# Layer 1's projections, scores and compressed scores in two scaled F16 parts instead of two F32R parts

## The chip, the cores and the metric

The kernel runs on one core of a Trainium2 chip. The metric is the device time of one execution in microseconds; the time of a kernel is the median of its runs. One further execution is recorded by the profiler, and the profile's page and trace are of that one.

The core's engines run side by side, each in its own order, and wait for each other by semaphores: PE (matmul; its weight loads are listed as PEld), DVE (vector), ACT (activation functions and scaled copies), POOL (a second, general vector engine) and SP, which here issues the DMAs. PE writes only into PSUM, eight banks of 128 partitions x 512 F32 numbers; DVE and ACT empty them.

## The reference

Two layers over x of 1024 positions and 1024 channels, each `x <- x + W_out(mixer(RMSNorm(x)) * silu(z))`, then a final RMSNorm. Layer 0 is an attention with a forget gate (16 heads of 64 channels, causal). Layer 1, the one that is changed, has 16 query heads in 4 groups that share keys and values, and three branches, mixed by a sigmoid gate:

```
proj = h @ w_in                  # q, and kc, vc, ks, vs, kw, vw of 4 x 64 each, 48 gates, z
kc, vc = compress(kc_raw), compress(vc_raw)          # 63 blocks, a small MLP with silu
p_c = softmax(mask(rope(q) . rope(kc) * 64**-0.5));  o_c = p_c @ vc
imp = overlap-sum of p_c over a group's heads;       idx = the 8 best blocks of 64 keys
o_s = softmax(rope(q) . ks over the chosen blocks) @ vs
o_w = softmax(rope(q) . kw over the last 512 keys) @ vw
y = ((g0*o_c + g1*o_s + g2*o_w) * silu(z)) @ W_out
```

## The kernel before

**Precision by parts.** A matrix product here is made of two parts of each operand: the high part is the value rounded to the product's type, the low part is what is left. `mm3` (line 134) issues three matmuls, high x high, high x low, low x high, one behind the other. In layer 0 and in layer 1's projections the parts are F32R, a form in which PE takes 32-bit operands in one pass. The products of the probabilities with the values are in F16 parts already.

**Layer 0** (to some 560 us). `merge` (line 212) interleaves two generators by costs written beside each step: the main one scores, softmaxes and multiplies tiles of 128 queries (`FoxDuo`), the fill projects the next head pair (`fox_k`, `fox_v`, `fox_q`, `fox_z`). Scores run two duos ahead of their products with the values; in between lies a DMA transpose of the probabilities.

**The passage** (some 560 to 640 us). `out_rest0` finishes the output projection for the last head pair, adds, normalizes with `gB` (the norm's gain) and writes the transposed h in its two parts, `hT` (`to_hT`, line 112), which layer 1's projections read.

**Sections** (some 610 to 960 us). Layer 1's weights are 28 sections of 1024 x 128: kc, qa, qr, vc, v, ka, kr, and z (8). `next_w` (line 777) loads two sections ahead through `load_w` (line 123): a DMA into a staging tile `wst` (one buffer), a cast to the high part on DVE, four subtractions for the low part on POOL. `section` (line 785) runs `project`, 24 matmuls of 512 columns a half, two halves, and hands each PSUM bank to a `use` function that empties it. q and k go as two stacked parts of 64 rows to DRAM (`qD`, `kD`, through `put_split`, line 901); `cmp_raw` keeps the raw compressed input in SBUF, `cmp_mlp` (line 818) makes the compressed keys `kcm` and values `vb`. `nsa_fill` (line 1156) lists the sections; `cmp_main` (line 1104) runs beside it by `merge`: 16 `cmp_unit`s (line 1057), each with 8 products of 128 columns, two DVE passes that add the mask, 8 exponentials, the block choice.

**Layer 1's attention** (some 960 to 1410 us). 32 `NsaSuper`s (16 heads x 2 halves of the queries). A `unit` (line 1320) makes one score tile of 128 queries: up to 1024 keys for the chosen blocks (y = 0), up to 640 for the window (y = 1). PE writes it (line 1343), DVE adds the mask and takes the row's minimum in one instruction (line 1350; the scores are negated), ACT takes the exponential (line 1353). The chosen blocks' probabilities are transposed by PE (line 1375) and split by ACT and DVE (lines 152 and 153), the window's are split on POOL (lines 1356, 1357) and transposed by DMA. PE multiplies both with the values (lines 1383 to 1385). The z sections and the first part of the output projection are the fill.

The order on each engine follows the program's order where the planner finds a step ready, and lets a later one go first where it doesn't.

## Time and profile before

| | us |
|---|---|
| median of 3 runs | 1480.85 (1480.15 to 1482.15) |
| span of the profiled execution | 1477.9 |
| PE / PEld busy in it | 1402.7 / 1164.1 |
| DVE / ACT / POOL busy | 1064.7 / 805.7 / 594.0 |
| moved by DMA | 243.13 MB, 165 GB/s mean |

In the profile, a row of a group has the line, the engine, the operation, what it writes and reads, the shape, the count, then the busy time, the mean duration of one in ns, and the idle time before it with what ended it. A timeline row begins with the start in us from the span's start and the duration; rows of the same kind may be merged (x4). A PE duration is from the first column to the modelled end, so two that follow each other overlap; the distance between starts says what one costs. Windows give each engine's busy time in a stretch, its instructions in brackets, then the granted clock of PE, the share of the DMA engines and GB/s.

### The profile page before, as it was taken

How to read it: one execution, taken by the hardware profiler on the slowest of the kernel's cores; microseconds unless marked ns; L12 is line 12 of the kernel's file. 1: busy time of each engine (PE TensorE's matmuls, PEld its weight loads, DVE VectorE, ACT ScalarE, POOL GpSimd, SP SyncE). 2: the span in 40 equal slices, each digit the busy share in tenths (PEclk: the TensorE clock that was granted, in tenths of full speed). 3: DMA queues.
4: the chain of work that ended last, by engine and by line, in shares of the span. 5: the costliest groups of instructions: out<-in, count | busy, mean ns of one | idle time of the engine just before them, and what ended most of it. 6: DMA issues, size and time to landing. Idle time of an engine off the chain costs nothing.

```text
span 1477.9 us, 29812 instructions
## 1 busy us (share of the span) xinstructions
PE 1402.7 (95%) x10488; PEld 1164.1 (79%) x10488; DVE 1064.7 (72%) x2795; ACT 805.7 (55%) x2030; POOL 594.0 (40%) x781
## 2 busy tenths in 40 slices
PE   5999999999999898999999988989999999989998
PEld 4888888888888676877788867778888888877876
DVE  6586778787787787666554658768788878878744
ACT  5365646565565644344132565566676676766523
POOL 2233232333233220123433334357676766766400
PEclk9999999999999999999999998999999999999999
DMA  6886867877867987442525577686786786877534
GB/s 244 264 167 138 181 136 170 174 158 164 175 140 161 219 199 150 141 155 71 166 85 151 171 185 180 185 201 144 155 180 155 160 177 147 172 201 166 105 137 147
DMA packets 405557, 243.13 MB, mean 165 GB/s; under 512 B 332640, under 2 KB 352736, under 8 KB 405152
## 3 DMA queue, kind: packets, MB, share of 16 engines
q1 hardware_dynamic: 405408, 241.23, 67.9%
q8 instruction: 83, 1.36, 0.4%
q14 instruction: 66, 0.54, 0.1%
HBM read 121.36 MB, written 44.11 MB: 112 GB/s over the span
## 4 chain that ended last, share of the span: by engine, by line
PE 69%; DVE 13%; DMA 6%; ACT 6%; issue 3%; SPq 2%; POOL 1%; DVEq 0%; ACTq 0%; POOLq 0%
PE S_n L1343 6%; PE y L135 3%; PE ptp_n L1375 3%; PE y L137 3%; PE y L136 3%; PE k L135 2%; PE v L135 2%; PE k L136 2%; PE k L137 2%; PE S L597 2%; PE S L598 2%; PE v L137 2%; PE v L136 2%; PE O L631 2%; PE q L135 2%
## 5 line engine op out<-in xcount | busy, mean ns | idle before, releaser
L1353 ACT ACTIVATE P_n<-P_n,m_n 128x640 f32<-128x640 f32 (+7 forms) x256 | 187.4, 733 | 67.7 <-DVE m_n L1352 41.0
L615 ACT ACTIVATE P<-P,m 128x512 f32<-128x512 f32 (+1 forms) x192 | 116.8, 609 | 129.8 <-DVE m L606 128.9
L1343 PE MATMUL S_n<-nk,nq 128*128 128x320 f32 (+5 forms) x768 | 177.1, 345 | 11.0 <-DVE m_n L1350 7.9
L586 POOL TENSOR_TENSOR Bd<-B,tri 128x128 f32<-128x128 f32 x128 | 62.0, 500 | 232.8 <-DVE m L606 224.7
L1357 POOL TENSOR_TENSOR hl_n<-P_n,hl_n 128x640 f16<-128x640 f32 (+4 forms) x128 | 142.6, 1114 | 9.4
L1343 PEld LDWEIGHTS S_n<-nk,nq 128*128 128x128 f32 x768 | 125.0, 190 | 24.7 <-DVE m_n L1350 10.7
L617 DVE SCALAR_TENSOR_TENSOR hl<-P,hl 128x512 f16<-128x512 f32 (+1 forms) x192 | 114.7, 616 | 16.0 <-ACT hl L616 14.9
L1350 DVE CUSTOM_DVE_ANT_0 P_n<-S_n,wmask 128x640 f32<-128x640 f32 (+2 forms) x192 | 113.0, 595 | 18.4 <-PE S_n L1343 15.0
L1356 POOL CAST hl_n<-P_n 128x640 f16<-128x640 f32 (+4 forms) x128 | 75.2, 587 | 115.6 <-ACT P_n L1353 104.6
L152 ACT ACTIVATE pth_n<-ptp_n 128x512 f16<-128x512 f32 (+1 forms) x160 | 86.6, 546 | 55.2 <-PE ptp_n L1375 54.0
L153 DVE SCALAR_TENSOR_TENSOR ptl_n<-ptp_n,pth_n 128x512 f16<-128x512 f32 (+1 forms) x160 | 100.6, 634 | 18.5 <-ACT pth_n L152 17.0
L135 PE MATMUL y<-wo,ohi 128*128 128x512 f32 x230 | 93.9, 408 | 3.1 <-ACT ohi L499 1.4
L1375 PE MATMUL ptp_n<-ident,P_n 128*128 128x128 f32 x576 | 90.7, 278 | 5.7 <-DVE ptl_n L153 3.7
L616 ACT ACTIVATE hl<-P 128x512 f16<-128x512 f32 (+1 forms) x192 | 92.4, 513 | 2.3 <-DMA pT<-hl 1.0
L137 PE MATMUL y<-wo,olo 128*128 128x512 f32 x230 | 90.7, 394 | 0.0
L136 PE MATMUL y<-wo,ohi 128*128 128x512 f32 x230 | 90.2, 392 | 0.0
L1375 PEld LDWEIGHTS ptp_n<-ident,P_n 128*128 128x128 f32 x576 | 66.0, 141 | 19.0 <-DVE ptl_n L153 12.3
L1350 DVE CUSTOM_DVE_ANT_0 P_n<-S_n,bias 128x640 f32<-128x640 f32 (+1 forms) x64 | 65.2, 1018 | 9.8 <-PE S_n L1343 9.7
L1383 PE MATMUL O_n<-nv,pth_n 128*128 128x64 f16 x576 | 70.3, 195 | 0.5
L597 PE MATMUL S<-KH,Q 128*128 128x512 f32 (+1 forms) x192 | 64.2, 350 | 6.2 <-DVE m L606 6.2
L1384 PE MATMUL O_n<-nv,pth_n 128*128 128x64 f16 x576 | 69.5, 193 | 0.0
L1385 PE MATMUL O_n<-nv,ptl_n 128*128 128x64 f16 x576 | 68.5, 193 | 0.0
(395 smaller groups left out, 4543.9 us busy)
## 6 DMA issues: line engine op xcount, KB each, us to landing
nq<-qD SPq DMA_DIRECT2D x64, 256.0 KB
B<-cD SPq DMA_DIRECT2D x16, 512.0 KB
wo<-wD SPq DMA_DIRECT2D x16, 512.0 KB
nq<-qD SPq DMA_DIRECT2D x64, 128.0 KB
x<-in_x_dram SPq DMA_DIRECT2D x8, 512.0 KB
wst_k<-in_fox_w_dram SPq DMA_DIRECT2D x8, 512.0 KB
wst_v<-in_fox_w_dram SPq DMA_DIRECT2D x8, 512.0 KB
wD<-in_fox_w_out_dram SPq DMA_DIRECT2D x8, 512.0 KB
```

The source lines that it names most:

```text
L135: T.matmul(ps, wh, mh, start=first, stop=False, **kw)
L136: T.matmul(ps, wh, ml, start=False, stop=False, **kw)
L137: T.matmul(ps, wl, mh, start=False, stop=last, **kw)
L153: V.scalar_tensor_tensor(lo[:, 0:n], pt[:, 0:n], scale, h, OP.mult, OP.subtract)
L597: T.matmul(ps[:, 0:n], q, KH[j][:, k0:k0 + n], start=True, stop=False)
L615: A.activation(L[:, 0:n], L[:, 0:n], AF.Exp, bias=init, scale=-1.0, accum_out=self.lr[:, col + c:col + c + 1])
L617: V.scalar_tensor_tensor(lo[:, cs], L[:, 0:n], UP, hi[:, cs], OP.mult, OP.subtract)
L1343: T.matmul(ps[:, b, 0:w], self.q[x][:, qi * P:(qi + 1) * P], k[:, k0 + b * w:k0 + b * w + w], start=(x == 0), stop=(x == 1))
L1350: V.tensor_tensor_reduce(dst, src, mk, 1.0, 3e38, OP.add, OP.min, m)
L1353: A.activation(L, L, AF.Exp, bias=m, scale=-1.0, accum_out=self.l[:, y, qi:qi + 1])
L1357: G.tensor_tensor(hl[:, n:2 * n], L, hl[:, 0:n], OP.subtract)
L1375: T.transpose(pt[:, (x + i) * P:(x + i + 1) * P], L[:, kb * P - k0:(kb + 1) * P - k0], ident)
```

## The change

Layer 1's h, its projection weights, q, k, the compressed keys and the gate's weights become two F16 parts. F16 has a small range, so each group of weights (kc, vc, q, gate, then k, v, z) is first multiplied by a power of two that is derived from the sum of the group's squares; the norm's gain is scaled likewise, and the inverse factors go into the steps that empty PSUM, into the masks and into the exponentials.

- The sums of squares: `Squares` loads weights once more from DRAM, squares them on ACT and accumulates. `early` (25 tiles, of 512 columns at most, one buffer) steps after each half of `fox_q` and `fox_z` in layer 0; `late` (16 tiles of 1024 columns, two buffers) after each half of a section in layer 1. `step` first makes a [128, 1] copy that reads a tile of the surrounding work, so that the square can't run before it.
- `roots` adds the sums over the partitions by a small matmul with ones, and cuts the result to a power of two with integer operations on DVE. It runs after layer 0's attention, once more before the fifth qr section (`late_scales`), and once for the compressed keys, with a step of 2200 between their square and the root.
- `load_w` scales the staged weights in place on ACT, between the DMA and the cast; every second section is staged in another pool.
- The masks use 2**126 in place of 1e30.

```diff
+    class Squares:
...
+        def step(self, x):
+            if self.at:
+                t, col = self.at.pop(0)
+                z = consts.tile([P, 1], F32, tag="zg", bufs=2, name=f"zg_{col}")
+                A.activation(z, x, AF.Copy, scale=0.0)
+                A.activation(t, t, AF.Square, bias=z, accum_out=sums[:, col:col + 1])
+            self.load()
+
+    def roots(groups, name, parts=P):
...
+        for i, x in enumerate(groups):
+            V.tensor_reduce(r[:, 0, i:i + 1], x, AX.X, OP.add)
+        V.tensor_copy(tb[:, 0:n], r[:, 0])
+        V.tensor_copy(tb[:, n:2 * n], r[:, 0])
+        pt = ps_t(f"total_{name}")
+        T.matmul(pt[:, 0:2 * n], ones, tb, start=True, stop=True)
+        V.tensor_scalar(r[:, 0].bitcast(I32), pt[:, 0:n].bitcast(I32), 24, 23,
+                        OP.logical_shift_right, OP.logical_shift_left)
+        V.tensor_scalar(r[:, 1].bitcast(I32), r[:, 0].bitcast(I32), 0x3F800000, None, OP.bitwise_xor)
+        return r
...
-    def load_w(pool, src, name, cols=P):
-        st = pool.tile([P, KC, cols], F32, tag="wst", bufs=1, name=f"wst_{name}")
+    def load_w(pool, src, name, scale=None, staged=None):
+        st = (staged or pool).tile([P, KC, P], F32, tag="wst", bufs=1, name=f"wst_{name}")
         dma(st, src)
-        hi = pool.tile([P, KC, cols], F32R, tag="whi", bufs=2, name=f"whi_{name}")
-        lo = pool.tile([P, KC, cols], F32R, tag="wlo", bufs=2, name=f"wlo_{name}")
+        dt = F32R if scale is None else F16
+        hi = pool.tile([P, KC, P], dt, tag="whi", bufs=2, name=f"whi_{name}")
+        lo = pool.tile([P, KC, P], dt, tag="wlo", bufs=2, name=f"wlo_{name}")
+        if scale is not None:
+            A.activation(st, st, AF.Copy, scale=scale)
         V.tensor_copy(hi, st)
...
             ready["q", p, half] = Q
+            early.step(f(q[:, 0:1]))
...
             ready["z", p, half] = zs
+            early.step(z[:, 0:1])
...
     merge(fox_main(), fox_fill(), PACE, rebase=True, cap=4000)
+    r1 = roots([sums[:, 0:4], sums[:, 4:8], sums[:, 8:24], sums[:, 24:25]], "early")
...
         dma(gB, a["norm_g"][1:2, :].to_broadcast([P, D]))
+        gain.extend(gain_scale(gB))
...
-    hT = [[h1.tile([P, KC, 512], F32R, tag=f"h{x}{i}", name=f"hT1_{x}_{i}") for i in range(2)] for x in range(2)]
+    hT = [[h1.tile([P, KC, 512], F16, tag=f"h{x}{i}", name=f"hT1_{x}_{i}") for i in range(2)] for x in range(2)]
...
-    qD = dram.tile([H, 2, P, 512], F32, name="qD")
-    kD = dram.tile([8, P, S], F32, name="kD")
+    qD = dram.tile([H, 2, P, 512], F16, name="qD")
+    kD = dram.tile([8, P, S], F16, name="kD")
...
                 pts.append(use(half, pt, len(pts)))
+                late.step(pt[:, 0:1])
+
+    late = Squares(pa, [(a["nsa_w"][i], 13 + i) for i in range(12, 28)], D, 2)
...
-                A.copy(R[0:64, g, half * 512:half * 512 + 512], pt[r, :])
+                A.activation(R[0:64, g, half * 512:half * 512 + 512], pt[r, :], AF.Copy, scale=E[kind][r])
...
+            A.activation(t2, t1, AF.Square, accum_out=ks[0:64])
+            yield 2200
+            r = roots([ks], "kcm")
...
-        V.tensor_tensor(L, sc[:, :, :, 1, :], cmask[:, t0:t0 + 2, None, :].to_broadcast([P, 2, 4, 64]), OP.add)
-        V.tensor_tensor(L, sc[:, :, :, 0, :], L, OP.add)
+        uc = ready["uc"]
+        for y in range(2):
+            V.scalar_tensor_tensor(L[:, y], sc[:, y, :, 1, :], uc, cmask[:, t0 + y, None, :].to_broadcast([P, 4, 64]),
+                                   OP.mult, OP.add)
+        V.scalar_tensor_tensor(L8, sc.rearrange("p y r a c -> p (y r) a c")[:, :, 0, :], uc, L8, OP.mult, OP.add)
...
-            V.tensor_tensor_reduce(dst, src, mk, 1.0, 3e38, OP.add, OP.min, m)
+            unit, minus = ready["units"][0:2]
+            V.tensor_tensor_reduce(dst, src, mk, 1.0 if y else unit, 3e38, OP.add, OP.min, m)
             if y:
-                V.tensor_scalar(m, m, LNUP, None, OP.add)
-            A.activation(L, L, AF.Exp, bias=m, scale=-1.0, accum_out=self.l[:, y, qi:qi + 1])
+                V.tensor_scalar(m, m, unit, LNUP, OP.mult, OP.add)
+            A.activation(L, L, AF.Exp, bias=m, scale=minus if y else -1.0, accum_out=self.l[:, y, qi:qi + 1])
```

More of the change, by code (lines that the diff above doesn't have):

```diff
@@ L30 @@
 BIG = 1e30
+FAR = 2.0 ** 126
 SCALE = HD ** -0.5
@@ L74, in tile_fox_nsa, with silu2 @@
     G.memset(zero, 0.0)
+    ones = consts.tile([P, P], BF16, name="ones")
+    G.tensor_copy(ones, warm.to_broadcast([P, P]))
     wp = ctx.enter_context(tc.tile_pool(name="wp", bufs=2))
     ready = {}
-    def silu2(dst, src):
-        A.activation(dst, src, AF.Tanh, scale=0.5)
+    def silu2(dst, src, scale=0.5):
+        A.activation(dst, src, AF.Tanh, scale=scale)
         V.scalar_tensor_tensor(dst, dst, 1.0, src, OP.add, OP.mult)
@@ new lines, in roots @@
+    def roots(groups, name, parts=P):
+        n = len(groups)
+        r = consts.tile([P, 4, n], F32, name=f"roots_{name}")
+        tb = consts.tile([P, 2 * n], BF16, name=f"sb_{name}")
+        for i, x in enumerate(groups):
[8 more added lines that the diff above has]
+        return r
@@ new lines, in gain_scale @@
+    def gain_scale(gB):
+        u = consts.tile([P, 4], F32, name="gain")
+        m, r, e, b = (u[:, i:i + 1] for i in range(4))
+        V.tensor_reduce(m, gB, AX.X, OP.max, apply_absolute_value=True)
+        V.tensor_scalar(m, m, 2.0 ** -60, None, OP.max)
+        V.tensor_scalar(m.bitcast(I32), m.bitcast(I32), 0x7F800000, None, OP.bitwise_and)
+        V.tensor_scalar(r.bitcast(I32), m.bitcast(I32), 0x7F800000, None, OP.bitwise_xor)
+        V.tensor_scalar(gB, gB, r, 2.0 ** 8, OP.mult, OP.mult)
+        V.tensor_scalar(e, m, 2.0 ** -9, None, OP.mult)
+        V.tensor_scalar(b, r, 2.0 ** 15, 2.0, OP.min, OP.mult)
+        return e, b
@@ L743, in tile_fox_nsa, with scales, bound @@
     out_rest0(ow, ready["wout"], after0)
+    W, E = {}, {}
+    def scales(r, kinds, name):
+        V.tensor_scalar(r[:, 2], r[:, 1], 2.0 ** 77, None, OP.mult)
+        V.tensor_scalar(r[:, 3], r[:, 0], gain[0], 2.0 ** 50, OP.mult, OP.mult)
+        for i, x in enumerate(kinds):
+            W[x], E[x] = r[:, 2, i:i + 1], r[:, 3, i:i + 1]
+    def bound(n, e, sign, name):
+        u = consts.tile([P, 2], F32, name=f"bound_{name}")
+        V.tensor_scalar(u[:, 0:1], n, 2.0 ** 68, 2.0 ** 25, OP.mult, OP.min)
+        V.tensor_tensor(u[:, 0:1], u[:, 0:1], gain[1], OP.mult)
+        V.tensor_scalar(u[:, 1:2], u[:, 0:1], e, sign, OP.mult, OP.mult)
+        return u[:, 0:1], u[:, 1:2]
+    scales(r1, ("kc", "vc", "q", "g"), "early")
+    rq, eq = bound(r1[:, 1, 2:3], E["q"], -1.0, "q")
     ow.release()
@@ L793, in section, with late_scales @@
                 pts.append(use(half, pt, len(pts)))
+                late.step(pt[:, 0:1])
+    late = Squares(pa, [(a["nsa_w"][i], 13 + i) for i in range(12, 28)], D, 2)
+    late.load()
+    def late_scales():
+        r = roots([sums[:, 25:29], sums[:, 29:33], sums[:, 33:41]], "late")
+        scales(r, "kvz", "late")
+        rk, ek = bound(r[:, 1, 0:1], E["k"], 1.0, "k")
+        u = pers.tile([P, 4], F32, name="units")
+        inverse(u[:, 0:1], rq, rk, SCALE)
+        V.tensor_scalar(u[:, 1:2], u[:, 0:1], -1.0, None, OP.mult)
+        V.tensor_scalar(u[:, 2:3], E["z"], 0.5, None, OP.mult)
+        V.tensor_tensor(u[:, 3:4], E["z"], E["v"], OP.mult)
+        ready["units"] = [u[:, i:i + 1] for i in range(4)]
+        ready["ek"] = ek
     pm = tc.alloc_tile_pool(name="pm", bufs=1, reuse_waits="tile")
@@ L954, in use @@
             x = rt(f"kx_{half}")
-            A.copy(x, pt)
+            A.activation(x, pt, AF.Copy, scale=ready["ek"])
             rope(x[0:64], x[64:128], rows[0], rows[1], 64, 1.0, half, k_dst, "k")
@@ L1009, in gate_sec @@
                 yield 430
-            A.copy(gT[half], pt[64:112, :])
-            V.tensor_tensor(gT[half], pt[0:48, :], gT[half], OP.add)
+            A.activation(gT[half], pt[64:112, :], AF.Copy, scale=E["g"][64:112])
+            V.scalar_tensor_tensor(gT[half], pt[0:48, :], E["g"][0:48], gT[half], OP.mult, OP.add)
         pt = ps_t("pgt")
@@ L1044, in load_q12 @@
         if (h, s) not in Q12:
-            q = [kv[1 - s].tile([P, 512], F32R, tag=f"nq{i}", name=f"nq{i}_{h}_{s}") for i in range(2)]
-            dma(f(q[0]), qD[h, s])
+            q = [kv[1 - s].tile([P, 512], F16, tag=f"nq{i}", name=f"nq{i}_{h}_{s}") for i in range(2)]
+            dma(q[0], qD[h, s])
             for i in range(2):
-                dma(f(q[1][rows[i], :]), qD[h, s, rows[1 - i], :])
+                dma(q[1][rows[i], :], qD[h, s, rows[1 - i], :])
             Q12[h, s] = q
```

87 lines of the change are left out of this document (57 added, 30 removed).

## The prediction

> **What bounds the kernel now.** I read the page from the top, then busy time by stage, then the chain of waits, then TensorE's instructions one by one. A busy share says little of PE here, because the records of two matmuls overlap; the last of these views decides.
>
> ```profile
> span 1477.9 us, 29812 instructions
> ...
> PE 1402.7 (95%) x10488; PEld 1164.1 (79%) x10488; DVE 1064.7 (72%) x2795; ACT 805.7 (55%) x2030; POOL 594.0 (40%) x781
> ...
> PE 69%; DVE 13%; DMA 6%; ACT 6%; issue 3%; SPq 2%; POOL 1%; DVEq 0%; ACTq 0%; POOLq 0%
> ```
>
> The first two lines are the busy times; the third, the chain that ended last, goes through PE for 69% of the span. By stage (start:end, then PE, PEld, DVE, ACT, POOL busy, clock, DMA share, GB/s):
>
> ```profile
> 90.00:540.00 450.00, 442.88 (x2787) 363.84 (x2784) 347.62 (x1066) 255.54 (x638) 143.03 (x223) 0.99 0.78 169
> 540.00:640.00 100.00, 91.52 (x541) 73.74 (x539) 72.09 (x177) 45.80 (x116) 12.05 (x20) 1.00 0.59 154
> 640.00:800.00 160.00, 155.63 (x773) 129.91 (x772) 85.46 (x150) 49.71 (x78) 58.92 (x75) 0.99 0.38 117
> 800.00:960.00 160.00, 147.25 (x724) 121.30 (x722) 109.92 (x255) 87.43 (x344) 60.97 (x77) 0.97 0.65 179
> 960.00:1410.00 450.00, 430.11 (x5052) 364.44 (x5052) 361.41 (x965) 301.78 (x712) 294.63 (x349) 1.00 0.75 162
> ```
>
> These are layer 0's attention, the passage between the layers, layer 1's first sections, its later sections with the compressed scores, and layer 1's attention. What a wide matmul costs PE is the step from start to start (start, duration, engine, line, ...):
>
> ```profile
> 596.28 0.39 PE L135 MATMUL y<-wo,ohi 128*128 128x512 f32 x1
> 596.51 0.39 PE L136 MATMUL y<-wo,ohi 128*128 128x512 f32 x1
> ...
> 607.61 0.39 PE L137 MATMUL y<-wo,olo 128*128 128x512 f32 x1
> ```
>
> From 596.28 to 607.61 lie 50 steps, so 227 ns for 512 columns, with no hole. Where such steps follow each other, PE is the limit, and only a shorter step helps. If I give each of the 773, 724 and 5052 matmuls of the last three rows the step that its form shows back to back, the steps fill some 97%, 89% and 90% of these stages. So the changed part of the program is bound by PE's order, except around the compressed scores.
>
> **The change, part by part.** Half the width of an operand does not halve the step: 0.44 ns a column is already one column after another. What F16 costs is seen in the kernel's own F16 products:
>
> ```profile
> 302.52 0.23 PE L631 MATMUL O<-v,pT 128*128 128x128 f16 x1
> 302.58 0.19 PE L632 MATMUL O<-v,pT 128*128 128x64 f16 x1
> 302.61 0.22 PE L631 MATMUL O<-v,pT 128*128 128x128 f16 x1
> ...
> 1152.47 0.19 PE L1384 MATMUL O_n<-nv,pth_n 128*128 128x64 f16 x1
> 1152.49 0.19 PE L1385 MATMUL O_n<-nv,ptl_n 128*128 128x64 f16 x1
> 1152.52 0.48 PE L135 MATMUL nz<-hT,whi_nz 128*128 128x512 f32 x1
> 1152.84 0.40 PE L136 MATMUL nz<-hT,whi_nz 128*128 128x512 f32 x1
> 1153.07 0.40 PE L137 MATMUL nz<-hT,wlo_nz 128*128 128x512 f32 x1
> ```
>
> 128 and 64 columns take 60 and 30 ns, weight load included. No F16 product of 512 columns stands in the trace, so its step is bounded: four times the F16 step of 128 columns (57 to 60 ns) is no gain at all, 213 ns (a gain of 14) if the whole extra of the F32 step is not per column. I take a gain of 8 ns. The Trainium skill, "TensorE: Matmul & The Clock Gate", section "Back-to-back issue gap", gives 518 cycles for 512 columns, 216 ns; by it the gain would be 11 ns and the sum below 4 us shorter. The same section's other figure, 131 ns sustained at 512, disagrees with the 227 ns here; it is a rival below.
>
> The second gain is larger. The nz product at 1152.52 follows short ones, and its successor starts 320 ns later in place of 227: its F32 weights could not be loaded behind a matmul of 30 ns. F16 weights are loaded at every 30 ns step above. The same shows in the scores, first behind a wide product, then behind a transpose:
>
> ```profile
> 999.99 0.76 PE L1343 MATMUL S_n<-nk,nq 128*128 128x320 f32 x4
> ...
> 1151.47 0.85 PE L1343 MATMUL S_n<-nk,nq 128*128 128x320 f32 x4
> ...
> 971.61 0.47 PE L1343 MATMUL S_n<-nk,nq 128*128 128x448 f32 x1 [0.41 <-DVE m_n L1350]
> ...
> 1391.81 0.70 PE L1343 MATMUL S_n<-nk,nq 128*128 128x512 f32 x2
> ...
> 957.44 0.47 PE L135 MATMUL nz<-hT,whi_nz 128*128 128x512 f32 x1
> ...
> 1317.91 0.48 PE L135 MATMUL nz<-hT,whi_nz 128*128 128x512 f32 x1
> ```
>
> The same four matmuls take 0.85 in place of 0.76. I count 124 such scores (first and last: the third and fourth line) and 94 such nz products (the last two), 18.6 us together. Scores of 128 columns (64 of them in attention, 128 compressed ones) also pay for the F32 load, about 107 ns a step:
>
> ```profile
> 817.95 1.00 PE L1063 MATMUL sc<-kcm,nq 128*128 128x128 f32 x8
> 818.79 0.45 PE L135 MATMUL pn_v<-hT,whi_nv 128*128 128x512 f32 x1
> ```
>
> Eight in 0.84 us, 105 each, against 57.
>
> *Attention, 960 to 1410.* Offered on PE: 18.6 of loads, 704 scores x 8 ns = 5.6, 64 narrow ones x 50 = 3.2, z products 384 x 8 = 3.1: 30.5 us, 7% of the stage. Against it stands DVE. Its mask-and-minimum for the chosen blocks gets a per-partition scalar, and so does the small step behind the window's. What such an operand costs is shown by layer 0's same instruction with and without one:
>
> ```profile
> L606 DVE CUSTOM_DVE_ANT_0 P<-S,Bd,m 128x128 f32<-128x128 f32 x84 | 27.4, 348 | 1.8
> ...
> L606 DVE CUSTOM_DVE_ANT_0 P<-S,Bd 128x128 f32<-128x128 f32 x27 | 7.7, 284 | 1.7 <-PE S L598 1.6
> ```
>
> 64 ns, so 256 x 0.06 = 15 us: DVE goes from 361 to 377 us of work. With all 30.5 us saved that would be 90% of the stage, and DVE is already full in parts of every round of heads:
>
> ```profile
> 1126.00:1132.00 6.00, 6.00 (x79) 5.53 (x78) 6.00 (x14) 4.75 (x10) 4.80 (x5) 1.00 0.46 87
> ...
> 1230.00:1236.00 6.00, 6.00 (x79) 5.56 (x78) 6.00 (x14) 4.77 (x10) 4.81 (x5) 1.00 0.39 58
> ```
>
> DVE is busy 6.00 of 6.00. In those parts a faster PE only waits for its score banks. I take 70% of the offer: **-21** (from -8 to -31).
>
> *Sections, 640 to 960.* 20 sections of 48 products and the gate's 32 x 8 ns = 7.9, the compressed scores 128 x 48 ns = 6.2. Part of it falls where PE already waits for the softmax of the compressed scores; the compressed score's two DVE passes become three with scalars, 16 x some 0.3 us in that chain. I take half: **-7**. New on ACT: each section's weights are multiplied by their scale (1024 columns), and 16 squares of 1024 columns; per instruction:
>
> ```profile
> L94 ACT ACTIVATE h_n<-xr 128x512 f32<-128x512 f32 x32 | 20.0, 626 | 29.7 <-DVE xr L1476 16.5 <-DVE xr L720 12.9 <-DVE st_n L102 0.4
> ...
> L94 ACT ACTIVATE h_n<-x 128x1024 f32<-128x1024 f32 x8 | 8.5, 1060 | 4.6 <-DMA x<-in_x_dram 4.6
> ...
> L985 ACT ACTIVATE nvT<-nvT,nvsc 128x512 f32<-128x512 f32 x8 | 5.5, 716 | 8.6 <-DVE nvsc L179 8.6
> L986 ACT CAST nvs<-nvT 128x512 f16<-128x512 f32 x8 | 4.7, 609 | 1.3 <-DMA nv<-nvs 1.3
> ```
>
> 1.06 us for 1024 columns, and 107 ns more with a scalar per partition (716 against 609). 20 x 1.17 + 16 x 1.4 is 46 us on an engine with 183 us idle in these 320; it lies beside PE. Where it is ahead of an eviction or a compression input in ACT's order, PE waits a little: **+2** (0 to +10). Behind a square, SP's next load waits for its buffer; the weights have a second staging buffer now, which takes that wait away. The late roots' matmul waits on DVE in PE's order, but the squares it needs end two sections before. The compressed key's new square and root (some 3 us) have one section's products put between them.
>
> *Layer 0.* 25 squares of 512 columns: 0.63, about 0.19 for the accumulator read and 0.2 for the ordering copy, 25 us on ACT, which is idle for 195 of the 450. Each ordering copy waits for a q or z tile that DVE finishes; behind it on ACT stand the exponentials of the running scores. 25 loads of 256 KB are 6.5 MB, 9% more than the stage moves (169 GB/s x 450 us), and each load waits on SP for the square before it (one buffer), with the probabilities' transposes behind it on SP; those have two tiles' time to land. **+3** (0 to +25).
>
> *Passage.* The first roots (nine tiny DVE steps) and the gain's scale (some 3 us of DVE) lie where DVE idles; the products and the ACT scaling ahead of layer 1's first weights can show: **+1.5** (0 to +6).
>
> *At nothing:* q and k in F16 halve two kinds of load, 64 x 256 and 64 x 128 KB,
>
> ```profile
> nq<-qD SPq DMA_DIRECT2D x64, 256.0 KB
> ...
> nq<-qD SPq DMA_DIRECT2D x64, 128.0 KB
> ```
>
> which are ahead of their use in nearly all rounds; the cover is the round before. The masks and the windows' exponentials with a second scalar (128 x 0.1 us) lie on ACT, idle for a third of the stage.
>
> The sum: -21 - 7 + 2 + 3 + 1.5 = -21.5, on the median of 1480.85 (the span is 1477.9, some 3 us of each run lie outside it and don't change): **1459 us**.
>
> **Rivals.** *All of it:* the wide step gains 11 to 14 ns and DVE keeps up: -31 - 14 and some 8 for the step, nothing added: about 1428. For it: PE's chain share; against it: DVE's full windows. *DVE takes over:* attention gives 8 us only, the sum is 1472; for it DVE at 84% of the old stage and full in bursts; against it, it is idle for 16%. *Slower, by layer 0's squares:* in ACT's strict order each ordering copy holds the exponentials until DVE has finished its tile, about 1 us, then 1.0 of new work. If two thirds of that 2.1 reach PE at 25 places, +35 in place of +3: 1491. It decides from about 1 us a place (25 us eat the gain). Against it: in 90 to 540 the scores run two tiles ahead of their products. *The change doesn't do it:* F16 neither steps nor loads faster in these forms; only the added work is left, +6.5, about 1487. Against it: the 30 ns steps. *Much faster:* wide F16 products step faster than one column at 0.44 ns, 131 ns by the page named above; 1376 projections x 96 ns are 132 us, DVE would stop it near 1400. Against it: 57 ns for 128 columns.
>
> **How the numbers follow.** Forecast 0.48 (its own range 1447 to 1468), all of it 0.10, DVE takes over 0.25, squares in layer 0 0.12, no effect 0.04, much faster 0.01. The range leaves out the slow case and most of the two fast ones: 1437 to 1481. 0.2% is 3 us, about what this kernel's measurement can tell from no change. Faster: 0.48 + 0.10 + 0.01 + 0.21 of DVE's 0.25 = 0.80; same: the other 0.04 of it; slower: 0.12 + 0.04 = 0.16.
>
> **What would show it.** Steps of 512 columns at 216 to 223 ns in the sections; successors of nz products behind short ones at the same step; DVE's share in attention at 85 to 88%, and DVE as the releaser of scores more often; 90 to 540 as long as before within 3 us. I am wrong if layer 0 grows by more, if wide steps stay at 227, or if PE's holes in attention grow by as much as its steps shrink.

## The result, and the profile after

| | before | after |
|---|---|---|
| median (from to) | 1481.08 (1480.15 to 1482.15) | 1490.49 (1486.92 to 1491.52) |
| ratio | | 1.0057 [1.0043, 1.0070] |
| span of the profiled execution | 1477.9 | 1485.1 |

Slower by 9 us, where 21.5 less was forecast. The page's first lines, as those shown of before:

```profile
span 1485.1 us, 30100 instructions
...
PE 1376.8 (93%) x10491; PEld 996.4 (67%) x10491; DVE 1078.4 (73%) x2860; ACT 893.1 (60%) x2183; POOL 585.4 (39%) x783
```

PE has 26 us less to do and its weight loads 168 us less, and yet the span is longer: PE waits more. Now the single steps. A timeline of PE in layer 1's attention, where a z product stands behind products of 30 ns:

```profile
1091.09 0.19 PE L1516 MATMUL O_n<-nv,hT_n 128*128 128x64 f16 x1
1091.12 0.38 PE L204 MATMUL nz<-hT,whi_nz 128*128 128x512 f16 x1
1091.34 0.38 PE L205 MATMUL nz<-hT,whi_nz 128*128 128x512 f16 x1
1091.55 0.38 PE L206 MATMUL nz<-hT,wlo_nz 128*128 128x512 f16 x1
1091.77 0.38 PE L204 MATMUL nz<-hT,whi_nz 128*128 128x512 f16 x1
```

The successor of the first z product starts 220 ns later, as all others do (the three steps from 1091.12 to 1091.77 are 217 ns each), where before it took 320. So both gains that were worked out on PE are there. The stages, in the columns of the table of stages before:

```profile
90.00:540.00 450.00, 444.11 (x2773) 361.62 (x2772) 347.25 (x1066) 277.41 (x707) 144.53 (x224) 0.99 0.82 181
540.00:640.00 100.00, 93.62 (x546) 74.92 (x545) 71.26 (x191) 43.86 (x109) 5.85 (x12) 1.00 0.57 144
640.00:800.00 160.00, 145.44 (x705) 77.94 (x705) 88.50 (x164) 84.19 (x143) 55.93 (x75) 0.94 0.48 153
800.00:960.00 160.00, 140.69 (x770) 74.71 (x769) 102.47 (x264) 98.47 (x340) 55.94 (x75) 0.98 0.52 132
960.00:1410.00 450.00, 411.60 (x5028) 292.32 (x5028) 377.34 (x993) 321.09 (x737) 295.88 (x356) 0.98 0.68 141
```

In the third row PE does 705 matmuls in the time of 773, in the last 5028 in that of 5052, at steps that are shorter: no engine is full there, and PE's share has fallen. The windows cut the program at fixed times. Where the time goes is read from landmarks of the work itself, the first or last matmul of a kind. Before, in us, and then the difference to it in the profiled execution of after and of the kernels below that the argument needs:

| landmark | before | after | e1 | e5 | e13 | e17 | e16 |
|---|---|---|---|---|---|---|---|
| end of layer 0: its last y product | 632.0 | +5.4 | +1.8 | -0.3 | +1.0 | +7.0 | +6.7 |
| first product of layer 1 | 637.8 | +12.2 | +8.9 | +1.5 | +2.8 | +14.1 | +6.7 |
| first score of layer 1's attention | 962.4 | +9.2 | +7.2 | -3.0 | -10.5 | -1.4 | +8.8 |
| last score | 1395.1 | +7.1 | +3.5 | -6.5 | -25.4 | -12.1 | +10.5 |
| end | 1477.9 | +7.2 | +3.6 | -6.4 | -25.3 | -12.0 | +10.5 |

So of after: layer 0 loses 5.4, the passage 6.8 more, the sections gain 3.0, attention 2.1 in place of 21. Against this, the four heads 8 to 11, in which no wait for a weight falls, go from 104.0 to 98.2 us (heads are counted from 0, each from its first score to the next head's first score): 5.8 of the 7.6 that a quarter of the stage was offered (30.5 / 4). There the gain is made. Three heads lose it again: head 0 takes 4.1 us more than before, head 2 2.6 more, head 13 3.9 more. PE's holes (idle times of over 0.4 us that the profile shows ahead of a matmul) from 960 to 1420 sum to 33.2 us, before to 14.9. So they grow by 18.3 us, about as much as PE's busy time in the stage shrinks (430.1 to 411.6): the last of the signs of being wrong that the prediction named.

**Where attention loses it.** The timeline of after at the hole in head 2 (in brackets: idle time ahead, and what ended it):

```profile
1043.73 0.53 SPq L128 DMA_DIRECT2D wst_nz<-in_nsa_w_dram  x1
...
1044.28 0.18 ACT L1484 ACTIVATION_READ_ACCUMULATOR P_n<-P_n,m_n 128x1 f32 x1
...
1047.72 1.15 ACT L133 ACTIVATE wst_nz<-wst_nz,roots_late 128x1024 f32<-128x1024 f32 x1 [3.25 <-DMA wst_nz<-in_nsa_w_dram]
1048.77 0.58 ACT L221 ACTIVATE pth_n<-ptp_n 128x512 f16<-128x512 f32 x1
...
1049.38 0.69 DVE L222 SCALAR_TENSOR_TENSOR ptl_n<-ptp_n,pth_n 128x512 f16<-128x512 f32 x1 [3.22 <-ACT pth_n L221]
...
1050.13 0.69 PE L1506 MATMUL ptp_n<-ident,P_n 128*128 128x128 f32 x2 [2.69 <-DVE ptl_n L222]
...
1130.54 0.69 DVE L134 CAST whi_nz<-wst_nz 128x1024 f16<-128x1024 f32 x1
```

The scaling (L133) stands in ACT's order ahead of its data: the load was issued at 1043.73, ACT is free at 1044.46 and stands still until 1047.72. Behind it is the split of the probabilities (L221), behind that DVE's half of the split, behind that PE, which stands still for 2.69 us. The weights that ACT waits for are cast only at 1130.54, over 80 us later: nothing needed them then. The same wait comes with most sections (18 of the 28 scalings). ACT's groups of after from 598 on (busy, mean ns | idle time just before, and what ended it):

```profile
L133 ACT ACTIVATE wst_nz<-wst_nz,roots_late 128x1024 f32<-128x1024 f32 x8 | 9.2, 1151 | 14.2 <-DMA wst_nz<-in_nsa_w_dram 14.2
L133 ACT ACTIVATE wst_nqr<-wst_nqr,roots_early 128x1024 f32<-128x1024 f32 x6 | 6.9, 1146 | 11.5 <-DMA wst_nqr<-in_nsa_w_dram 11.4
L133 ACT ACTIVATE wst_nv<-wst_nv,roots_late 128x1024 f32<-128x1024 f32 x4 | 4.6, 1150 | 21.2 <-DMA wst_nv<-in_nsa_w_dram 18.4 <-DVE bound_k L835 2.8
...
L133 ACT ACTIVATE wst_nvc<-wst_nvc,roots_early 128x1024 f32<-128x1024 f32 x2 | 2.3, 1150 | 7.6 <-DMA wst_nvc<-in_nsa_w_dram 7.6
```

These and two small groups more make 53 us in which ACT waits for a DMA: 8 of them in attention (three waits, at 1047, 1093 and 1139), 45 in the sections. One scaling itself takes 1.15 us, as the forecast had it (1.17).

The largest hole of after, 6.03 us at 1313 in head 13, stands behind a wait of the same kind in a step that both kernels have, the cast of the output projection's weights:

```profile
1315.96 1.14 ACT L624 CAST wo<-wo 128x512 fp32r<-128x512 f32 x2 [6.35 <-DMA wo<-wD]
```

Before, that wait is 3.39 us and its hole 2.39. Why it is longer in after was not traced.

### The profile page after: what moved, and what is told of

Its sections match the earlier page's. It is cut to its first block, busy times and chain, and to the rows that moved or that the text cites. A ratio compares the mean times of both kernels' runs of the same rounds, so it can differ in the third digit from the quotient of the medians.

```text
span 1485.1 us, 30100 instructions
## 1 busy us (share of the span) xinstructions
PE 1376.8 (93%) x10491; PEld 996.4 (67%) x10491; DVE 1078.4 (73%) x2860; ACT 893.1 (60%) x2183; POOL 585.4 (39%) x783
## 5 line engine op out<-in xcount | busy, mean ns | idle before, releaser
L1473 PE MATMUL S_n<-nk,nq 128*128 128x320 f16 (+5 forms) x768 | 156.0, 318 | 19.8 <-DVE m_n L1481 17.1
L1484 ACT ACTIVATE P_n<-P_n,m_n,units 128x640 f32<-128x640 f32 (+4 forms) x128 | 100.4, 784 | 32.7 <-DVE m_n L1483 31.7
L1484 ACT ACTIVATE P_n<-P_n,m_n 128x640 f32<-128x640 f32 (+7 forms) x128 | 98.5, 770 | 28.5 <-DVE m_n L1481 27.8
L1473 PEld LDWEIGHTS <-nq 128*128 128x128 f16 x768 | 71.5, 99 | 64.8 <-issue 24.5
L222 DVE SCALAR_TENSOR_TENSOR ptl_n<-ptp_n,pth_n 128x512 f16<-128x512 f32 (+1 forms) x160 | 100.2, 633 | 15.3 <-ACT pth_n L221 14.1
L221 ACT ACTIVATE pth_n<-ptp_n 128x512 f16<-128x512 f32 (+1 forms) x160 | 85.9, 545 | 36.1 <-PE ptp_n L1506 35.0
L1506 PE MATMUL ptp_n<-ident,P_n 128*128 128x128 f32 x576 | 93.9, 280 | 11.0 <-DVE ptl_n L222 5.9
L1481 DVE CUSTOM_DVE_ANT_0 P_n<-S_n,wmask 128x640 f32<-128x640 f32 (+4 forms) x128 | 83.4, 652 | 8.8 <-PE S_n L1473 7.7
L1481 DVE CUSTOM_DVE_ANT_0 P_n<-S_n,bias,units 128x640 f32<-128x640 f32 (+1 forms) x64 | 68.9, 1077 | 8.4 <-PE S_n L1473 6.2
```

The lines of the kernel that those rows point to most:

```text
L222: V.scalar_tensor_tensor(lo[:, 0:n], pt[:, 0:n], scale, h, OP.mult, OP.subtract)
L1473: T.matmul(ps[:, b, 0:w], self.q[x][:, qi * P:(qi + 1) * P], k[:, k0 + b * w:k0 + b * w + w], start=(x == 0), stop=(x == 1))
L1481: V.tensor_tensor_reduce(dst, src, mk, 1.0 if y else unit, 3e38, OP.add, OP.min, m)
L1484: A.activation(L, L, AF.Exp, bias=m, scale=minus if y else -1.0, accum_out=self.l[:, y, qi:qi + 1])
L1506: T.transpose(pt[:, (x + i) * P:(x + i + 1) * P], L[:, kb * P - k0:(kb + 1) * P - k0], ident)
```

## The experiments

Each ratio is to runs of the kernel before that were taken with it; their medians lie between 1480.55 and 1482.45, so small differences between rows are better read from the ratios. The theories: **A**, that layer 0 grew by where the constants now push its weights (here PE's stationary operand: `whi` and `wlo`, and `ohi` and `olo` in the y products); **B**, ACT's wait, above; **C**, that layer 1's first weights come late for the memory that they are staged in; **D**, the squares; **E**, that the masks hold DVE at the start of attention; **F**, DVE's scalar operands, which the prediction had as what may take over.

| | median | ratio [95%] |
|---|---|---|
| e1_place | 1482.40 | 0.9997 [0.9983, 1.0010] |
| e2_scale_off_act | 1501.26 | 1.0126 [1.0104, 1.0148] |
| e3_no_early_squares | 1485.98 | 1.0033 [1.0021, 1.0046] |
| e4_before_plus_copy | 1521.86 | 1.0270 [1.0257, 1.0284] |
| e5_first_stage | 1473.28 | 0.9935 [0.9923, 0.9948] |
| e6_load_ahead | 1479.70 | 0.9984 [0.9972, 0.9995] |
| e7_both | 1472.60 | 0.9936 [0.9923, 0.9948] |
| e8_no_late_squares | 1476.20 | 0.9954 [0.9941, 0.9967] |
| e9_masks_on_pool | 1471.16 | 0.9938 [0.9917, 0.9958] |
| e10_no_scalar_operands | 1481.21 | 0.9999 [0.9982, 1.0017] |
| e11_squares_in_layer_0 | 1482.90 | 1.0013 [0.9999, 1.0026] |
| e12_all_mended | 1482.89 | 1.0006 [0.9989, 1.0022] |
| e13_scale_held | 1455.88 | 0.9837 [0.9817, 0.9856] |
| e14_no_scaling | 1448.23 | 0.9778 [0.9762, 0.9793] |
| e15_held_no_operands | 1449.98 | 0.9794 [0.9776, 0.9811] |
| e16_before_other_place | 1489.10 | 1.0050 [1.0034, 1.0067] |
| e17_held_alone | 1464.33 | 0.9882 [0.9864, 0.9901] |
| e18_held_no_squares | 1452.74 | 0.9802 [0.9782, 0.9822] |

### Layer 0: squares or place

**e3** leaves out the early squares (their sums are set to 1, so the weights of kc, vc, q and the gate are not scaled by their size):

```diff
+    early.items = []
+    G.memset(sums[:, 0:25], 1.0)
```

**e1** keeps the squares and moves the late small tiles out of the constants, so that all that layer 0 allocates behind them comes to lie 128 bytes lower; before had them at 21728, after at 22624, e1 at 22496 of each partition, which is 768 above before, a multiple of 256:

```diff
+    spare = consts.tile([P, 24], F32, name="spare")
...
-        r = consts.tile([P, 4, n], F32, name=f"roots_{name}")
+        r = pool.tile([P, 4, n], F32, name=f"roots_{name}")
...
```

> The changed kernel with 128 bytes less in the pool of constants (small tiles of the late roots go elsewhere, 96 bytes are added), so that layer 0's weights lie at the same place modulo 256 bytes as before; nothing that layer 0 computes or loads changes. Theory A, place: in the changed kernel the wide F32 steps of layer 0 take 232 ns from the first microseconds on, ahead of the first square, against 227 to 231 before, and all other forms keep their step; so the extra 4.8 us of layer 0 come from where its operands lie. Then the steps go back to 227 to 231 and the last transpose of layer 0 comes about 5 us earlier: 1485 in place of 1490. Rival, the squares' work and loads: the steps stay at 232 and layer 0 keeps its 4.8 us.

> The changed kernel without the 25 early loads, copies and squares: their sums are set to 1, so the early scales are others than those of the reference's weights. Theory A: layer 0 keeps its 4.8 us, as the squares lie beside PE: the time is within 1.5 us of the changed kernel. Rival, the squares hold ACT or the queue of loads: layer 0 loses 4 to 5 us.

e3's layer 0 stays long: its k products lie 1.0 us earlier than after's from the 49th on and just as much at the last (460.1 and 461.1), and its last y product comes 3.1 us later. So in these two executions the 25 squares, their copies and their loads slow nothing down one by one. But e3's median is 4.5 us lower than after's, and its profiled execution (1491.76) is the slowest of its nine, so what the early squares cost in all stays open. e1 keeps them and is 8 us faster than after; the profiled executions show 3.6 of these 8 (the landmarks), all by the end of layer 0. What differs is the step of F32R products of 512 columns. In after, two products of one stretch without a hole, 61 steps apart:

```profile
598.53 0.39 PE L205 MATMUL y<-wo,ohi 128*128 128x512 f32 x1
...
612.70 0.39 PE L206 MATMUL y<-wo,olo 128*128 128x512 f32 x1
```

14.17 us, 232 ns a step. The same 61 steps in e1:

```profile
595.66 0.40 PE L207 MATMUL y<-wo,ohi 128*128 128x512 f32 x1
...
609.51 0.39 PE L208 MATMUL y<-wo,olo 128*128 128x512 f32 x1
```

13.85 us, 227 ns, as before the change. **e16** is the test from the other side: the kernel before, with 384 unused bytes among its constants, which puts the same weights where after has them modulo 256.

```diff
+    spare = consts.tile([P, 96], F32, name="spare")
+    G.memset(spare, 0.0)
```

> The kernel before with 384 unused bytes in the pool of constants, so that its weights lie at the place modulo 256 bytes that they have in the changed kernel; no instruction on the way is new. Theory A: its wide steps in layer 0 go from 227 to 232 ns and the time rises by 4 to 7 us, to 1485 to 1488. Rival: what e1 gave back was another thing; within 1 us of before.

Its 61 steps:

```profile
599.83 0.39 PE L138 MATMUL y<-wo,ohi 128*128 128x512 f32 x1
...
614.01 0.40 PE L139 MATMUL y<-wo,olo 128*128 128x512 f32 x1
```

14.18 us, 232 ns, and 8.5 us more in the median without any other change. Theory A holds: 384 unused bytes cost nearly as much as the whole change does. In layer 0, F16 products of 128 and 64 columns keep their steps in all of these kernels (medians of 57 and 28 ns), so it isn't the clock.

### The first weights of layer 1

In e1 the first product of layer 1 is still 8.9 us late. The loads, scaling, cast and product of after:

```profile
605.24 0.33 SPq L128 DMA_DIRECT2D wst_nkc<-in_nsa_w_dram  x1
...
637.81 0.33 SPq L128 DMA_DIRECT2D wst_nkc<-in_nsa_w_dram  x1
...
642.05 1.14 ACT L133 ACTIVATE wst_nkc<-wst_nkc,roots_early 128x1024 f32<-128x1024 f32 x1
...
648.87 1.28 DVE L134 CAST whi_nkc<-wst_nkc 128x1024 f16<-128x1024 f32 x2
...
649.98 0.63 PE L204 MATMUL pn_kc<-hT,whi_nkc 128*128 128x512 f16 x1
```

The second section's weights are loaded at 605, the first one's at 637.81: its staging tile (217024 to 221120 of a partition) lies in what layer 0's last output weights hold until their last product (212960 to 229344). **e5** exchanges the two staging pools, on e1:

```diff
-                                            W[kind if kind in W else kind[0]], pers if len(nq) % 2 else None)))
+                                            W[kind if kind in W else kind[0]], None if len(nq) % 2 else pers)))
```

> e1 with the two staging tiles exchanged, so that the first weights (kc 0) land in the old pool and not in the one whose memory layer 0's output weights still hold until their last product. Theory C, late first stage: in the changed kernel the first weights' load starts only after that product (637.8), their cast is at 648.9 and the first section starts behind the last transpose, where before it ran between the transposes; then the first section starts some 8 us earlier and 3 to 5 us of the time go, to about 1478. Rival: the casts come late because DVE is full of the norm's work, and nothing changes (within 1 us of e1).

```profile
600.15 0.33 SPq L128 DMA_DIRECT2D wst_nkc<-in_nsa_w_dram  x1
...
622.95 0.69 DVE L134 CAST whi_nkc<-wst_nkc 128x1024 f16<-128x1024 f32 x1
...
639.26 0.63 PE L206 MATMUL pn_kc<-hT,whi_nkc 128*128 128x512 f16 x1
```

The first weights are cast at 622.95, and the product at 639.26 comes 7.6 us behind layer 0's last one, where e1 has 12.9 and before 5.8. 9 us less than e1, 3 to 5 were expected: theory C holds.

### ACT's wait

**e2** takes the scaling off ACT: DVE's cast becomes a multiply, POOL scales for the low part.

```diff
-            A.activation(st, st, AF.Copy, scale=scale)
-        V.tensor_copy(hi, st)
+            V.tensor_scalar(hi, st, scale, None, OP.mult)
+            G.tensor_scalar(st, st, scale, None, OP.mult)
...
```

> The changed kernel with the weights' scaling taken off ACT: the high part is scaled by DVE as it is cast, and POOL scales the staged tile in place ahead of its subtractions. Theory B, ACT held: a scaling that stands in ACT's order waits for its own DMA (53 us of ACT's idle time), and the exponentials and splits behind it wait with it. Then the holes of PE in attention fall from 38 to 25 us or less, the half-clock stretches there from 17 to about 7 us, and the time by 8 to 15 us, to 1475 to 1482. Rival, DVE: the scalars per partition have filled DVE, and more work on it changes nothing or costs 2 us.

```profile
L134 POOL TENSOR_SCALAR wst_nz<-wst_nz,roots_late 128x1024 f32<-128x1024 f32 x8 | 22.8, 2852 | 14.3 <-DVE whi_nz L133 11.3 <-PE S_n L1475 1.6 <-DVE im L1227 1.4
```

On POOL a scaling takes 2.85 us, against ACT's 1.15, in a chain of cast, scaling and subtractions: the low parts come late, and 11 us are added to after. That is a new cost of its own; of ACT's wait it tells nothing.

**e4** does the one part alone on the kernel before: a copy in place on ACT for layer 1's weights, by a factor of 1.

```diff
+    unit = consts.tile([P, 1], F32, name="unit")
+    G.memset(unit, 1.0)
...
+        if name[0] == "n":
+            A.activation(st, st, AF.Copy, scale=unit)
```

> The kernel before, with one step of the change alone: layer 1's staged weights are multiplied by 1 on ACT, between their DMA and the cast, all else as before. Theory B: ACT waits for the weights' DMA here too, with exponentials behind it: slower by 6 to 15 us, with ACT idle for tens of us before these copies, and holes of PE behind them. Rival, ACT's work lies beside PE: 28 copies of 1.1 us change the time by less than 2 us.

```profile
L131 ACT ACTIVATE wst_nz<-wst_nz,unit 128x1024 f32<-128x1024 f32 x8 | 9.2, 1149 | 23.0 <-DMA wst_nz<-in_nsa_w_dram 23.0
```

+40 us. By the landmarks 6.4 of them lie in layer 0 (the constant for the factor moved its weights by 32 bytes: steps of 231 to 235 ns), 2.1 in the passage, 25.7 in the sections, where this kernel has one staging buffer, and 6.2 in attention. Copies of 1.15 us, with the waits ahead of them, can cost more than the change was to gain; this run doesn't part the copy from its wait.

**e6** loads each section's weights one section earlier, on e1; **e7** is e6 and e5.

```diff
...
+        st = (pers if len(nq) % 2 else wp).tile([P, KC, P], F32, tag="wst", bufs=1, name=f"wst_n{kind}{i}")
+        dma(st, a["nsa_w"][nsa_i[kind] + i])
+        sd.append((kind, i, st))
...
+        if key != ("kc", 0) and nq and not sd:
+            fetch()
```

> e1 with each section's load issued one section earlier (the second staging tile is free by then); the scaling stays on ACT at its place in the order. Theory B: ACT's wait for the weights' DMA (53 us before) falls below 15 us, the holes of PE in attention and the sections shrink, and the time falls by 8 to 15 us against e1, to 1467 to 1474. Rival, DVE or the order of ACT itself: ACT's waits go but what follows is late anyway; less than 3 us.

> e5 and e6 in one kernel. If B and C are separate, their gains add: 1464 to 1471, below both kernels of this study. If they are one delay counted twice, the time is that of the better of the two.

What ended ACT's idle time before the scalings of e6:

```profile
  DMA wst_nv<-in_nsa_w_dram: 18.1, 3
  DMA wst_nz<-in_nsa_w_dram: 13.8, 6
  DMA wst_nqr<-in_nsa_w_dram: 12.4, 4
```

The waits are those of after. Loads, and the scalings behind them, already ran as early as the staging tiles came free; written earlier, they run at the same place. So e6 took no wait away (2.7 us less than e1, with intervals that overlap), and e7 is e5 again.

**e13** moves the scaling itself. On e9 (below), the scaling gets a bias of zero that ACT makes from a tile of surrounding work, as `Squares.step` does, so that it can't be taken up before that work; by then the load has landed.

```diff
+    def note(x):
+        z = consts.tile([P, 1], F32, tag="hold", bufs=2, name="hold")
+        A.activation(z, x, AF.Copy, scale=0.0)
+        hold[:] = [z]
...
+                A.activation(st, st, AF.Identity, bias=hold[-1], scale=scale)
...
+                if half and key == keys[-1]:
+                    note(pt[:, 0:1])
...
+            if half:
+                note(z[:, 0:1])
```

**e14** is e9 with no scaling at all (the products are then too small or too large by the factors). **e17** is the hold alone: the kernel after with its own place of the weights, its own staging and its own masks.

> e9 with each section's scaling on ACT held until the first half of the section two before its use has been emptied, by a bias of zeros that is made from that half; the load itself stays as early. Theory B: ACT's waits for the weights' DMA (8 us in attention, 39 in the sections) fall below 10 us in all, the 2.7 us hole of the third head goes, and the time falls 3 to 6 us below e9, to 1465 to 1468. Rival: the waits of ACT lie in time that nobody misses, but for the one hole; less than 2 us.

> e9 without the scaling of the staged weights: layer 1 computes with weights that are too small by their scales. Theory B: what the scaling on ACT costs in all, waits and work, 4 to 8 us against e9, and no more than 2 us below e13 if e13's waits are gone. Rival: within 2 us of e9.

> The changed kernel, its weights in layer 0 at the same place modulo 256 bytes as in it, with the scaling on ACT held as in e13 and nothing else mended. Theory B: the waits are a cost of their own, and 11 to 16 us go as between e9 and e13: 1474 to 1480, so that the change would have been no loss in spite of the other three costs. Rival: part of e13's gain came from what was mended before; less than 8 us.

ACT's groups of e13, and the window from 960 to 1410:

```profile
L141 ACT ACTIVATE wst_nz<-wst_nz,hold,roots_late 128x1024 f32<-128x1024 f32 x8 | 9.9, 1240 | 1.5 <-DMA wst_nz<-in_nsa_w_dram 1.3
L141 ACT ACTIVATE wst_nqr<-wst_nqr,hold,roots_early 128x1024 f32<-128x1024 f32 x6 | 7.4, 1234 | 0.4 <-DMA wst_nqr<-in_nsa_w_dram 0.2
L141 ACT ACTIVATE wst_nv<-wst_nv,hold,roots_late 128x1024 f32<-128x1024 f32 x4 | 4.9, 1240 | 0.2
```

```profile
960.00:1410.00 450.00, 424.08 (x5130) 308.84 (x5129) 371.55 (x964) 319.74 (x730) 289.87 (x345) 1.00 0.69 143
```

The 44 us of idle time before these three groups are 2 (over all groups 53 are 5; the copies that hold the scalings wait 5 us for DVE instead), and the clock granted is 1.00, not 0.98. Attention (first to last score) is 14.9 us shorter than before, where after's is 2.1. In time: -15 us on e9 (3 to 6 were expected), and alone on the kernel after -26 us, from 1490.49 to 1464.33 (11 to 16 were expected). Of what e14 shows as the price of all scaling (-23 on e9), 15 were the wait. PE's holes of over 0.4 us from 960 to 1420 fall from 33.2 to 22.0 in e17 and 20.1 in e13. Most of the gain lies ahead of attention, though: of the 19.2 us between the profiled executions of after and e17, the sections give 12.5 and attention 8.6 (layer 0 and the passage are 1.9 longer). ACT's idle time is not itself the price: e8, below, has 67 us of it ahead of its scalings, e1 55, and e8 is the faster by 6 us.

### Masks, DVE's operands, late squares

At the start of attention, the timeline of after:

```profile
977.50 0.69 DVE L134 CAST whi_nz<-wst_nz 128x1024 f16<-128x1024 f32 x1 [3.80 <-PE nz L205]
...
978.97 0.22 DVE L1412 TENSOR_SCALAR wmask<-tri 128x128 bf16<-128x128 f32 x1
979.11 0.69 DVE L1413 TENSOR_SCALAR wmask<-tri 128x128 bf16<-128x128 f32 x1
979.73 1.50 DVE L1418 COPY bias<-wmask 128x128 bf16<-128x128 bf16 x4
...
982.08 1.14 PE L1473 MATMUL S_n<-nk,nq 128*128 128x384 f16 x3 [4.47 <-DVE m_n L1481]
```

The masks stand behind a cast that waits 3.80 us for its buffer, and the scores behind the masks; before, the masks ran at 960 to 961, ahead of that cast. **e9** makes them on POOL, on e5:

```diff
-    V.tensor_scalar(wmask[:, 0:P], tri, 0.0, FAR, OP.is_equal, OP.mult)
+    G.tensor_scalar(wmask[:, 0:P], tri, 0.0, FAR, OP.is_equal, OP.mult)
...
```

> e5 with the masks of layer 1's attention built on POOL in place of DVE. Theory E: at the start of attention DVE stands behind a weights' cast that waits 3.8 us for PE, then builds the masks in a chain (2.2 us), and PE's first scores wait 4.5 us and fall to half clock; the masks belonged to what I costed at nothing. With POOL building them some 3 us go: 1470 to 1471, and the hole ahead of the second group of scores falls from 4.6 to about 2 us. Rival: the cast alone makes the wait; less than 1 us.

The hole before the second group of scores goes from 4.47 (e5) to 2.31 us. The median falls by 2, but so does that of the kernel before beside it: the ratios, 0.9935 and 0.9938, are the same. Theory E's place is right; that it costs time is not shown. In e17, with the masks still on DVE, the hold alone takes this hole to 3.09 us and head 0 from 4.1 us above before to 0.8.

**e10** (on e5) and **e15** (on e13) give DVE's two steps the constant that the scalar has for these weights, so no per-partition operand:

```diff
-            V.tensor_tensor_reduce(dst, src, mk, 1.0 if y else unit, 3e38, OP.add, OP.min, m)
+            V.tensor_tensor_reduce(dst, src, mk, 1.0 if y else 2.0 ** -7, 3e38, OP.add, OP.min, m)
             if y:
-                V.tensor_scalar(m, m, unit, LNUP, OP.mult, OP.add)
+                V.tensor_scalar(m, m, 2.0 ** -7, LNUP, OP.mult, OP.add)
```

> e5 with the unit of the scores as a constant in the two DVE steps of attention (2 to the -7, the value that these weights give), so that DVE reads no scalar per partition there; the results are the same. Theory F, DVE takes over: the operands cost DVE 64 x 0.06 + 64 x 0.06 + 128 x 0.06 us or some 15 us in attention, DVE stands at 88 to 89% of the steady heads, and half or more of it reaches the end: 6 to 10 us faster than e5, 1463 to 1467. Rival: the operands lie in DVE's idle time, less than 2 us.

> e13 with the unit of the scores as a constant in DVE's two steps, as in e10; the results are the same. Theory F, DVE takes over: DVE has 15 us less to do in attention and 6 us or more reach the end. Rival: PE's order bounds the steady heads and DVE's operands are covered; within 2 us of e13.

e10 came out 8 us slower than e5, where 6 to 10 less were expected. Its profiled execution, its fastest, shows 3.8 of them, and a wait of ACT at a new place, in head 4, which takes 32.2 us (26.5 in e5):

```profile
1087.85 1.15 ACT L133 ACTIVATE wst_nz<-wst_nz,roots_late 128x1024 f32<-128x1024 f32 x1 [5.56 <-DMA wst_nz<-in_nsa_w_dram]
```

With that wait gone the question can be put. The same window of mid attention in e13 and then in e15:

```profile
1100.00:1280.00 180.00, 171.57 (x2270) 123.97 (x2267) 155.08 (x420) 137.16 (x315) 128.11 (x158) 1.00 0.72 142
```

```profile
1100.00:1280.00 180.00, 173.83 (x2262) 124.28 (x2259) 149.51 (x418) 134.89 (x313) 129.15 (x157) 1.00 0.72 151
```

DVE has 5.6 us less to do in 180 (15 in the stage, as estimated), but attention is shorter by 17.7 - 14.9 = 2.8 us only. The rest of the 6 us between the medians lies for the most part in sections whose code is the same (3.2 us). So DVE's operands are not what holds attention back.

**e8** (on e1) leaves out the late squares, **e18** (on e13) all squares (their sums set to 1). **e11** (on e5) takes the late squares in layer 0, with the early ones. **e12** puts e6, e9 and e11 together.

```diff
-    late.load()
+    late.items = []
+    G.memset(sums[:, 25:41], 1.0)
```

```diff
+                    + [(a["nsa_w"][i][:, 4 * x:4 * x + 4, :], 2 * i + 1 + x) for i in range(12, 28) for x in range(2)], 512, 1)
...
```

> e1 without the 16 late loads, copies and squares (the late sums are set to 1, about their true value). Theory D: each square waits on ACT for its own load, and SP's queue holds the weights' loads behind those of the squares, which wait for a free buffer; the sections give back 3 to 8 us and ACT's waits for weights in the sections shrink. Rival: they lie beside PE as the early ones do, less than 2 us.

> e13 without any of the 41 loads, copies and squares (the sums are set to 1). Theory D, the late squares cost 4 to 6 us by themselves: 1450 to 1452. Rival: what e8 gave back was ACT's wait for the weights behind them, which is gone in e13; within 2 us of e13.

> e5 with the 16 late squares moved into layer 0, as 32 more tiles of 512 columns behind the halves of the keys and values there; the sections have no squares left. The early squares cost nothing (e3: layer 0 keeps its time to 0.1 us from end to end), the late ones some 6 us (e8). If both hold, 1467 to 1469. Rival: 57 loads and squares are too much for layer 0's queue, and it loses what the sections gain: 1473 or more.

> e9 and e11 with the weights' loads one section ahead (e6): the change with its side costs mended. If the side costs are separate, 1473 less 3 (masks), 5 (late squares) and 0 to 2 (loads): 1463 to 1466, some 1% below the kernel before. If they hide behind each other, no better than the best of e9 and e11.

Without late squares 6 us go on e1, without any squares 3 on e13 (there the intervals overlap, and e18's layer 0 ends 2.1 us earlier than e13's). 32 more squares in layer 0 are not free: its end is 9.7 us later than before, 10.0 later than in e5, and the sections gain 1.0 against e5. e12 is a miss: its layer 0 ends 10.9 us later than before, and there is a wait of ACT of 4.97 us in attention besides.

## Why the prediction was wrong, step by step

- **PE's shorter steps** were right in mechanism. The wide step is 216 to 217 ns, a gain of 11 where 8 was taken. The Trainium skill's 216 ns ("TensorE: Matmul & The Clock Gate", section "Back-to-back issue gap"), which it gives for a product by itself, agrees with the rows at 1091; the same section's sustained 131 ns was not seen in any run (the shortest step of such a product is 214 ns). The successor of a wide product behind short ones no longer waits for its weights, and steady heads give 2.9 us a pair.
- **The step that failed**: the scaling on ACT, "it lies beside PE ... PE waits a little: +2 (0 to +10)". The size of the work was right (1.15 us each), and ACT is idle for two fifths of the span. But the cost is not its time: the scaling stands in a queue that runs in order, ahead of its data, and holds the exponentials, splits and evictions that PE needs next. The prediction had no term for ACT's wait for the load, and for the scalings in attention no term at all; between the profiled executions of after and e17 lie 12.5 us in the sections, where it had +2, and 8.6 in attention, where it had nothing. The second staging buffer was counted on against waits of the loads; against this one it doesn't help, since the load into it begins only when it comes free and the scaling is queued at once behind it (e6). The Trainium skill states that ScalarE's queue is strictly first in, first out (the same page, section "Architectural detail: the array is 16× 32×32, not 1× 128×128"); the trace agrees, with L221 behind L133 at 1048.77. The prediction applied that very rule, with the wait, to the squares in layer 0, and to the scaling only with its work. Price: 26 us alone (e17), 15 once the rest is mended (e13). With the hold alone the change gives 1464.33, in the forecast's own range of 1447 to 1468, by luck in part: layer 0 and the passage are then 14.1 us longer than before (+4.5 was forecast), the sections 15.4 shorter (5), attention 10.7 shorter (21).
- **Layer 0, "+3"** came near the measured +5.4 for a wrong reason. Most of it is the place of the weights, which no step foresaw: with all squares and the old place, layer 0 ends at +1.8 (e1), -0.3 (e5) and +1.0 (e13), with the new place and no change else at +6.7 (e16). So the rival "slower, by layer 0's squares" had the sign right and the cause wrong; that its 1491 is the time measured is luck.
- **The passage, "+1.5 (0 to +6)"**, was 6.8: not the scaling ahead of the first weights, but the memory in which they are staged (e5; the passage is then +1.8).
- **The sections, -7**, could show only once the wait was gone: first product to first score gives -3.0 in after, -13.3 in e13. That is near the whole of what was offered there, not half: with steps of 216 ns, an estimate of 992 x 11 + 128 x 48 ns = 17 us.
- **Attention, -21**, gives -14.9 with the wait gone, inside the range taken, and still below the 70% that was taken of the offer. **DVE takes over** was not what held the rest: without the operands 2.8 us come (e15).
- **The masks "at nothing"** lengthen a hole of PE by 2.2 us (4.47 in e5, 2.31 in e9), which the time doesn't show: they were moved behind a cast that waits, which the prediction did not look at.

The prices don't add up to one sum: the same hold is worth 26 or 15 us, probably because waits hide each other, which no run shows by itself. In the order tried they go 1490.49, 1482.40 (place), 1473.28 (first stage), 1471.16 (masks), 1455.88 (hold), as ratios 1.0057, 0.9997, 0.9935, 0.9938, 0.9837. That last kernel, e13, computes all that the change computes and is 25 us faster than before; e15 is faster still, but its constant holds for these weights alone. What e13's attention still lacks lies in part in heads 12 and 13 (60.2 us before, 61.6 in e13, while heads 8 to 11 are 5.2 shorter): there ACT casts the output projection's weights, again in place and ahead of their data. In before and in e13:

```profile
1307.07 1.14 ACT L550 CAST wo<-wo 128x512 fp32r<-128x512 f32 x2 [3.39 <-DMA wo<-wD]
```

```profile
1283.95 1.14 ACT L636 CAST wo<-wo 128x512 fp32r<-128x512 f32 x2 [4.30 <-DMA wo<-wD]
```

The kernel before thus had a wait of this very kind, in its own trace. It was not tried without it. Open as well is the order that the planner finds: kernels that differ in one line come out some 3 us apart in sections that they share.

## What to carry to other kernels

An in-place step on data from a DMA can cost its engine the rest of the DMA's latency, and all that is queued behind it waits as well: price it by its place in the queue and by what stands there, not by the engine's idle share, and tie it to work that surely comes after the landing. When a change adds or moves tiles, compare the addresses of untouched operands and what the new tile's memory held before; a step in code that the diff doesn't touch can change. And look for the gain in a stretch without the suspected wait (here the four heads in mid attention) before doubting the mechanism.

## What the runs showed of the hardware that was not expected

- F32R products of 512 columns take 227 or 232 ns by where their weights lie relative to the moving operand: at one place 227 (before, e1), 128 bytes off 232 (after, e16), 32 bytes off 231 to 235 (e4). In the output projection of layer 1, where both operands moved by the same bytes, all of these kernels have 227 (medians from 1420 on). F16 products showed nothing of it. Three places were tried; why it is so is not known.
- A hole of PE of a few us was paid twice. The two windows of after around the hole at 1047:

```profile
1047.00:1050.50 3.50, 0.81 (x15) 0.69 (x14) 1.12 (x2) 2.69 (x5) 1.61 (x3) 0.85 0.92 127
1050.50:1054.00 3.50, 3.50 (x27) 2.02 (x26) 2.00 (x7) 1.40 (x4) 0.64 (x1) 0.66 0.47 127
```

PE is full again in the second, at a granted clock of 0.66. That adds about 1.2 us (a third of 3.5) to a hole of 2.7. Behind the holes of 4.47 us at 977 and 6.03 us at 1313 the clock is 0.50 in the 3.5 us from 982 and from 1319.
- One scaling of 1024 columns in place takes POOL 2.85 us, ACT 1.15 (e2, after).
